# A recurrence with PSUM tiles of its own for even and odd steps, and fewer PSUM banks for the dense products and the preparation

## The chip, the core and the metric

The kernel runs on one NeuronCore of one Trainium2 chip. The metric is device time in microseconds (us) of one execution, inputs and outputs in HBM. The five engines are TensorE (PE, matrix products), VectorE (DVE), ScalarE (ACT), GpSimdE (POOL) and SyncE (SP, which issues DMAs here). Matrix products land in PSUM, which this kernel uses as eight banks of 128 partitions x 512 fp32 values, one tile per bank.

## The reference, cut to what matters

Two requests of 512 tokens and width 1024 go through the same two layers. Layer 0 is dilated window attention beside a Hyena convolution, then a feed-forward layer with a width-3 convolution (`ffn`, 2816 wide). Layer 1 is a bidirectional RWKV-7 recurrence, then another `ffn`. The recurrence is the part that the change is about:

```
def _wkv_scan(r, decay, k, v, kk, a, reverse):
    def step(S, inp):
        r_t, w_t, k_t, v_t, kk_t, a_t = inp
        sa = jnp.einsum('bhvk,bhk->bhv', S, -kk_t)
        S = (S * w_t[:, :, None, :] + sa[..., None] * (kk_t * a_t)[:, :, None, :]
             + v_t[..., None] * k_t[:, :, None, :])
        return S, jnp.einsum('bhvk,bhk->bhv', S, r_t)
...
x = x + g1 * mix
h = _rmsnorm(x, p['norm2']) * (1.0 + sc2) + sh2
x = x + g2 * _conv_ffn(h, p)
```

## The kernel before, in words

The two requests are two Python generators, a (s = 0) and b (s = 1), that are woven by `run` with fixed weights. While a is in its recurrence (`rw_loop`), b supplies dense products, and the other way round. From what the generators issue, a list scheduler makes one fixed order of instructions for each engine; it also decides which bank a tile gets. Instructions of an engine then run in that order, each waiting for what it needs.

**Dense products.** `dense` (L123) loads a block of weights, splits it into a high part (`whi`, an ACT cast, L107) and a low part (`wlo`, a POOL subtraction, L111), and accumulates 9 to 24 matmuls of 128x512 into one PSUM tile `pd`; ACT or DVE then read it. During the loops every three matmuls are followed by a yield, so that the recurrence's matmuls come in between.

**Recurrence.** The 512 tokens of a request are cut into 16 chunks of 32; both directions and up to two pairs of heads advance together. There are 72 steps for each request. A step of `rw_steps` (L1153) is a chain. First the state times the chunk's keys and queries (`X<-S,AR`) and a product of values (`X<-UV,Am`) go to PSUM. ACT takes `xs` from it (L1191), a product with the chunk's inverse (`X<-xs,Am`) follows, ACT takes `UV` (L1201). Then the outputs (`X<-UV,Am`) and the state's update (`X<-UV,TBK`) follow. DVE makes the new `S` from PSUM (L1212), and DVE or ACT copy the step's outputs into `Y` (L1221, L1223). All of this lives in one tile X of two banks: columns 0 to 255 hold the outputs, alternating by halves between even and odd steps, 256 to 383 the inverse's product, 384 to 511 the update. The framework orders two accesses of the same bank by different engines even where the columns differ, so the first product of the next step, `X<-S,AR`, waits for the `Y` copies of this one.

**Preparation.** `rw_front` makes the matrices of the next pair of heads: two PSUM tiles at a time for `Am` (`ps<-AR,BK`, read by DVE, L1075), then two for the transposes `TBK` (`ps<-ident,BK`, read by ACT, L1100). `rw_back` makes the inverse by 31 steps of two DVE instructions (L1125, L1127).

**Projection.** `rw_project` of a request ends in eight rounds (one for each block of 128 channels): a dense product `wv`, then products with low-rank weights, a gate (`ps<-lg1ah`, copied by ACT in L921), a transpose (`ps<-ident,tv`) and small products, each in a PSUM tile of its own. For b the last rounds come when a's loop is over. Its PSUM tiles then come from the same pool as the dense products.

**Banks before.** `psd` has three banks for the dense products, throughout. In mixer 0, `psm` has five. In a loop, `psl` has three and X two.

Of the kernel before, what the change touches and what calls it, by code (L numbers as in the profile page):

```python
# [8 lines left out]
F32 = mybir.dt.float32  # L9
F32R = mybir.dt.float32r  # L10
AF = mybir.ActivationFunctionType
ALU = mybir.AluOpType
AX = mybir.AxisListType
PSUM = bass.MemoryType.PSUM
# [3 lines left out]
L = 512  # L18
# [32 lines left out]
class K:  # L51
    def __init__(self, tc, a, outs):
        self.tc, self.nc, self.a, self.o = tc, tc.nc, a, outs
        self.ctx = ExitStack()
        self.side = ["left", "right"]
        self.grain, self.behind, self.last = KC, False, None

    def pool(self, name, bufs=1, space=None, ctx=None, side=None):
# [5 lines left out]
    def ps(self, name="ps"):  # L64
        pool = self.psm[self.cur] or self.psl or self.psd
        return pool.tile([128, 512], F32, tag="pd" if pool is self.psd else "ps", name=name)

    def v(self, name, i=0, n=1):
# [54 lines left out]
    def dense(self, src, nk, xs, evac, m=128, before=()):  # L123

        wh, wl = self.load_w(src, nk, m)
        ps = self.psd.tile([128, 512], F32, tag="pd", name="pd")
        for k in range(nk):
            self.mm3(ps[:m], (wh[k], wl[k]), xs(k), k == 0, k == nk - 1)
            if (k + 1) % self.grain == 0 and k + 1 < nk:
                yield self.grain * 648  # L130
        yield from before
        evac(ps[:m])
        yield (nk % self.grain or self.grain) * 648
# [13 lines left out]
    def setup(self):  # L147
        nc, a = self.nc, self.a
        self.cp = self.pool("const")
        self.wp = self.pool("w")  # L150
        self.psd = self.pool("psd", bufs=3, space=PSUM)
        self.dp = self.pool("dram", space=DRAM)
# [92 lines left out]
    def stat_end(self, s):  # L245

        nc = self.nc
        yield 3000
        ps = self.psd.tile([128, 512], F32, tag="pd", name="pd")
        for i in range(4):  # L250
            self.mm(ps[:, i:i + 1], self.r[s][:, i * 128:i * 128 + 128], self.ones[:, 0:1], start=True, stop=True)
        m = self.rc[s]
        nc.vector.tensor_scalar(m, ps[:, 0:4], 1.0 / D, 1e-6, ALU.mult, ALU.add)
        nc.gpsimd.tensor_tensor(m, m, self.mhalf[:, 0:4], ALU.pow)
        r3 = self.r[s].rearrange("p (i t) -> p i t", i=4)
        nc.vector.tensor_tensor(r3, self.ident[:, None, :].to_broadcast([128, 4, 128]), m[:, :, None].to_broadcast([128, 4, 128]), ALU.mult)
        yield 3000
        ps = self.psd.tile([128, 512], F32, tag="pd", name="pd")
        self.mm(ps, self.ones, self.r[s], start=True, stop=True)
        nc.scalar.copy(self.r[s], ps)  # L260
        yield 4000
# [177 lines left out]
    def attention(self, s, hs, ap, op, then, early):  # L439

        nc, a = self.nc, self.a
        xs = lambda k: hs[k]
# [8 lines left out]
        def project(g, hp):  # L451
            if hp == 0:
                V[g] = ap.tile([128, 4, 256], F32, tag="V", bufs=2, name="V")
                pv = [self.psd.tile([128, 512], F32, tag="pd", name="pv") for _ in range(2)]
                for i in range(2):
                    wh, wl = self.load_w(a["wva"][g, :, i * 4:i * 4 + 4], 4, 256)
                    for k0 in (0, 2):
                        for b in range(4):
                            o = pv[b // 2][:, b % 2 * 256:b % 2 * 256 + 256]
# [20 lines left out]
        g, hp = parts[-1]  # L480
# [249 lines left out]
    def rw_project(self, s, ctx):  # L730
        nc, a, side = self.nc, self.a, self.side[s]
        sc = lambda key, c: self.rwd[key, s][c]
        mp = self.pool(f"xm{s}", ctx=ctx, side=side)
        hsel = mp.tile([128, 2, 32], F32, name="hsel")
# [4 lines left out]
        o2 = self.pool(f"hid{s}", ctx=ctx, side=side)  # L739
        if s == 0:  # L740
            self.wq[0] = self.pool("wq", ctx=ctx, side=side)
            ctx.callback(lambda: self.wq.pop(0))
        c1 = ctx.enter_context(ExitStack())
        hp = self.pool(f"h1{s}", ctx=c1, side=side)
        o1 = self.pool(f"po{s}", ctx=c1, side=side)
# [14 lines left out]
        xx, xs = [], {}  # L760
# [40 lines left out]
        if s == 0:  # L801
            yield from differences(self.pool(f"xx{s}", ctx=c1, side=side))
        pn = self.psd.tile([128, 512], F32, tag="pd", name="pn")
        yield from mix(2)
# [4 lines left out]
        def k_evac(ps, c):  # L809
            while late:  # L810
                late.pop()()
            t = new("t1")
            nc.scalar.copy(t, ps)
            put("k", c, t)
            sq = new("t1")
            nc.scalar.activation(sq, ps, AF.Square, scale=self.v("kk", c))
            q = slice(c // 2 * 32, c // 2 * 32 + 32)
            late.append(lambda: self.mm(pn[q], hsel[:, c % 2], sq, start=c % 2 == 0, stop=c % 2 == 1))

# [121 lines left out]
    def rw_loop(self, s, ctx):  # L941

        nc, a = self.nc, self.a
        P = lambda n, b=1: self.pool(f"{n}{s}", bufs=b, ctx=ctx, side=self.side[s])
        self.psl = self.psm[s] = self.pool(f"psl{s}", bufs=3, space=PSUM, ctx=ctx, side=self.side[s])
        px = self.pool(f"pxu{s}", bufs=1, space=PSUM, ctx=ctx, side=self.side[s])
# [9 lines left out]
        NW = KC + NCH // WAVE - 1  # L956
        self.X = px.tile([128, 2, 512], F32, name="X")
        nc.vector.memset(self.X, 0.0)
        self.G = rc.tile([128, NW * WAVE, 2, 2], F32, name="G")
# [193 lines left out]
    def rw_steps(self, w, live):  # L1153
        nc, per, X = self.nc, self.per, self.X
        H = [slice(h * 64, h * 64 + 64) for h in range(2)]
# [12 lines left out]
        for i in range(WAVE):  # L1168
# [4 lines left out]
            for st in live:  # L1173
# [3 lines left out]
                us.append((st, m, d, st["c"] % 2, n, n // 2, n % 2))  # L1177
            V0 = tau % 2 * 128
            sv = lambda g: slice(V0 + g * 64, V0 + g * 64 + 64)
            uu = lambda g: slice(256 + g * 64, 320 + g * 64)  # L1180
            ss = lambda g: slice(384 + g * 64, 448 + g * 64)
            for st, m, d, g, n, j, q in us:
# [7 lines left out]
            xs = per.tile([128, 2, 2, 64], F32, tag="xs", bufs=1, name="xs")  # L1190
            nc.scalar.activation(xs, X[:, :, V0:V0 + 128].rearrange("p h (g v) -> p h g v", g=2), AF.Copy, scale=-1.0)  # L1191
            yield PW[6] * (1 if w < KC else PW[8] / 100)
# [18 lines left out]
            S = self.S = per.tile([128, 2, 2, 64], F32, tag="S", bufs=1, name="S")  # L1211
            nc.vector.tensor_tensor(S, X[:, :, 384:512].rearrange("p d (g v) -> p d g v", g=2), self.Sg, ALU.add)  # L1212
            Sg = self.Sg = per.tile([128, 2, 2, 64], F32, tag="Sg", bufs=1, name="Sg")
# [80 lines left out]
    def program(self):  # L1294
        self.setup()
        a, b = ((s, self.thread(s)) for s in range(NS))
        self.filter = self.hyena_filter()
# [11 lines left out]
        self.run((a, "wide", 45), (b, None, PW[0]))  # L1309
        self.run((a, "loop", 66), (b, None, PW[1]))  # L1310
        self.grain, self.behind = GRAIN, BEHIND
        self.run((a, "out1", 480), (b, "loop", PW[14], PW[2]))
        self.run((a, None, PW[3]), (b, "loop", 50))
        self.run((a, None, PW[4]), (b, "out1", 480))
        self.grain, self.behind = KC, False
        self.run((a, "end", PW[5]), (b, "normed", 59))
        self.run((b, "end", 1))
        self.ctx.close()

# [158 lines left out]
```

## Time and profile before

| what | value |
|---|---|
| median of 3 runs (3663.87 to 10453.56) | 3672.75 us |
| the profiled execution | 3673.42 us, span of the profile 3671.6 us |
| PE busy | 3349.3 us, 91% |
| DVE, ACT, POOL busy | 1839.7, 1586.2, 1599.1 us |
| granted TensorE clock, mean | 0.941 |
| recurrence of request a, of request b | about 1640 to 2324 us, 2560 to 3170 us |

Busy times are sums over an engine's instructions; an engine's wait is booked to the instruction that ended last before it. A clock of 1.00 is 2.4 GHz, 0.50 is 1.2 GHz.

### The profile page before, as it was taken

To read this page: it belongs to the slowest core of one execution; us is meant where nothing else is said; L and a number is where in the kernel's file an instruction comes from. 1 tells how busy PE (TensorE), PEld (TensorE's weight loads), DVE (VectorE), ACT (ScalarE), POOL (GpSimd) and SP (SyncE) were. 2 spreads that over 40 slices of the span, in tenths; PEclk is the share of its full clock that TensorE was granted. 3 is DMA by queue.
4 is the path that set the end of the run, shared out by engine and by line. 5 is a ranking of instruction groups with operands and counts; after the bars stand their busy time and mean duration, and the time that the engine had idled before them with its cause. 6 is when DMAs were issued, how large, how long until landed. Compare 5 with 4: busy or idle time off the path is not lost. (4 is left out here: it accounts for less than half of the span.)

```text
span 3671.6 us, 62184 instructions
## 1 busy us (share of the span) xinstructions
PE 3349.3 (91%) x24082; PEld 2390.4 (65%) x24082; DVE 1839.7 (50%) x3373; ACT 1586.2 (43%) x3233; POOL 1599.1 (44%) x1480
## 2 busy tenths in 40 slices
PE   7999999999998989988887888887988889989998
PEld 4555777877876766666665554555656566667776
DVE  5021432122336373577777777567777765442223
ACT  3122344443235445445545557544455454443332
POOL 2111343244446565444444456444444444444443
PEclk9999999999999999899988898798899999999999
DMA  7655231223243326543334331574334432342322
GB/s 247 224 181 198 67 112 64 69 81 122 76 149 115 119 82 207 197 128 95 102 98 134 101 102 48 199 256 129 100 89 106 113 77 83 110 164 89 97 90 88
DMA packets 335519, 450.62 MB, mean 123 GB/s; under 512 B 160023, under 2 KB 177687, under 8 KB 333816
## 3 DMA queue, kind: packets, MB, share of 16 engines
q1 hardware_dynamic: 259664, 235.16, 20.7%
q10 hardware_dynamic: 75560, 211.48, 17.9%
q8 instruction: 190, 3.11, 0.3%
q14 instruction: 105, 0.86, 0.1%
HBM read 373.92 MB, written 72.61 MB: 122 GB/s over the span
## 5 line engine op out<-in xcount | busy, mean ns | idle before, releaser
L111 POOL TENSOR_TENSOR wlo<-wraw,whi 128x512 fp32r<-128x512 f32 (+1 forms) x830 | 1087.5, 1314 | 1424.9 <-ACT whi L107 1218.5
L107 ACT CAST whi<-wraw 128x512 fp32r<-128x512 f32 (+1 forms) x830 | 497.5, 605 | 879.4 <-PE pd L77 648.8
L77 PE MATMUL pd<-midh,whi 128*128 128x512 f32 x704 | 294.7, 420 | 21.0 <-ACT midh L140 20.8
L77 PE MATMUL pd<-midl,whi 128*128 128x512 f32 x704 | 290.3, 413 | 5.3 <-DVE midl L143 4.8
L77 PE MATMUL pd<-midh,wlo 128*128 128x512 f32 x704 | 289.0, 411 | 0.3 <-POOL wlo L111 0.3
L327 DVE SCALAR_TENSOR_TENSOR x<-pd,ada,x 128x512 f32<-128x512 f32 x192 | 143.1, 748 | 209.4 <-PE pd L77 208.6
L77 PE MATMUL pd<-xml,whi 128*128 128x512 f32 (+1 forms) x448 | 194.1, 434 | 22.5 <-DVE xml L143 15.2
L77 PE MATMUL pd<-xmh,whi 128*128 128x512 f32 (+1 forms) x448 | 196.1, 441 | 6.1 <-ACT xmh L140 5.9
L1125 DVE TENSOR_TENSOR sub<-U,W 128x120 f32<-128x120 f32 (+7 forms) x496 | 186.4, 376 | 23.6 <-DMA U<-inv 11.2
L1127 DVE TENSOR_TENSOR W<-W,sub 128x120 f32<-128x120 f32 (+7 forms) x496 | 188.8, 381 | 12.4
L77 PE MATMUL pd<-xmh,wlo 128*128 128x512 f32 (+1 forms) x448 | 190.0, 425 | 1.3 <-POOL wlo L111 1.2
L77 PEld LDWEIGHTS pd<-midh,whi 128*128 128x128 f32 x704 | 136.4, 194 | 56.9 <-ACT midh L140 23.9
L1201 ACT COPY UV<-X 32x128 f32<-32x128 f32 x512 | 131.6, 257 | 85.1 <-PE X L77 54.2
L320 DVE TENSOR_TENSOR fa<-fa,pd 128x512 f32<-128x512 f32 x88 | 60.4, 686 | 214.4 <-PE pd L77 202.8
L290 DVE SCALAR_TENSOR_TENSOR fa<-pd,vecs,fa 128x511 f32<-128x511 f32 x88 | 65.8, 747 | 203.7 <-ACT fa L289 203.0
L1214 POOL TENSOR_TENSOR Sg<-S,G 128x256 f32<-128x256 f32 x144 | 94.7, 658 | 164.2 <-DVE S L1212 153.0
L77 PEld LDWEIGHTS pd<-midl,whi 128*128 128x128 f32 x704 | 137.4, 195 | 40.3 <-DVE midl L143 9.9
L77 PEld LDWEIGHTS pd<-midh,wlo 128*128 128x128 f32 x704 | 137.1, 195 | 32.7 <-POOL wlo L111 1.5
L77 PE MATMUL X<-UV,Am 32*32 32x64 f32 (+1 forms) x4096 | 129.0, 230 | 24.2 <-ACT UV L1201 22.1
L1223 ACT COPY Y<-X 32x128 f32<-32x128 f32 x256 | 65.7, 257 | 180.6 <-DVE Y L1221 98.9
L77 PEld LDWEIGHTS X<-UV,Am 32*32 32x32 f32 (+1 forms) x4096 | 79.9, 110 | 92.5 <-ACT UV L1201 67.1
L77 PE MATMUL X<-S,AR 64*64 64x64 f32 x1920 | 63.4, 241 | 83.9 <-ACT Y L1223 64.0
(474 smaller groups left out, 8066.2 us busy)
## 6 DMA issues: line engine op xcount, KB each, us to landing
wraw<-in_up ACTq DMA_DIRECT2D x176, 512.0 KB, 3.6
adaw<-in_adaw SPq DMA_DIRECT2D x96, 512.0 KB, 5.4
wraw<-in_dn ACTq DMA_DIRECT2D x128, 256.0 KB, 2.7
wraw<-in_win ACTq DMA_DIRECT2D x36, 512.0 KB, 3.7
x<-x SPq DMA_DIRECT2D x48, 256.0 KB, 3.8
wraw<-in_dn ACTq DMA_DIRECT2D x64, 192.0 KB, 2.4
x<-res SPq DMA_DIRECT2D x32, 256.0 KB, 3.0
wraw<-in_wk ACTq DMA_DIRECT2D x16, 512.0 KB, 3.8
```

The source lines that it names most:

```text
L77: return self.nc.tensor.matmul(*a, **k)
L107: nc.scalar.copy(h, raw[:, o:o + w])
L111: nc.gpsimd.tensor_tensor(l, raw[:, o + p:o + p + w2], h[:, p:p + w2].bitcast(F32), ALU.subtract)
L290: nc.vector.scalar_tensor_tensor(t[:, 1:], ps[:, :L - 1], w(0), t[:, 1:], ALU.mult, ALU.add)
L320: nc.vector.tensor_tensor(act, act, ps, ALU.mult)
L327: nc.vector.scalar_tensor_tensor(x[m], ps, self.ada[l][:, 40 + m, s:s + 1], x[m], ALU.mult, ALU.add)
L1125: nc.vector.tensor_tensor(w, U4[:, :, k:, e * K + k:e * K + k + 1].to_broadcast(shape), W4[:, e:e + 1, k:k + 1, 0:k + 1].to_broadcast(shap ...
L1127: nc.vector.tensor_tensor(W4[:, :, k:, 0:k + 1], W4[:, :, k:, 0:k + 1], w, ALU.add)
L1201: nc.scalar.copy(dst, X[ur, :, uu(g)])
L1214: nc.gpsimd.tensor_tensor(Sg, S, self.G[:, tau, :, :, None].to_broadcast([128, 2, 2, 64]), ALU.mult)
L1223: nc.scalar.copy(dst, src)
```

## The change

X becomes two tiles of two banks, used by even and odd steps (`X[tau % 2]`). To pay for these two banks, `psd` goes from three banks to two and `psl` from three to two. A third bank for dense products (`third`, `pd`) exists outside the stretch from the begin of a's loop to the begin of a's last `ffn`; in that stretch there is none. Where that bank is there, the dense products take it in every third turn. `pn`, the sums of squares of eight blocks, no longer keeps a PSUM bank during the `wk` products: it becomes an SBUF tile that is filled from short-lived PSUM tiles, by one ACT copy or one DVE addition of 32x512 for each block. In mixer 0 the two accumulators `pv` come from `psm` instead of `psd`. A pool `psn` of three banks serves request a's projection until its first part ends.

```
     def ps(self, name="ps"):
         pool = self.psm[self.cur] or self.psl or self.psd
...
+    def pd(self):
+        self.turn = (self.turn + 1) % 3
+        if self.psx and self.turn == 0:
+            return self.psx.tile([128, 512], F32, tag="px", name="pd")
+        return self.psd.tile([128, 512], F32, tag="pd", name="pd")
...
-        ps = self.psd.tile([128, 512], F32, tag="pd", name="pd")
+        ps = self.pd()
...
-        self.psd = self.pool("psd", bufs=3, space=PSUM)
+        self.psd = self.pool("psd", bufs=2, space=PSUM)
...
-                pv = [self.psd.tile([128, 512], F32, tag="pd", name="pv") for _ in range(2)]
+                pv = [self.ps("pv") for _ in range(2)]
...
+        self.psm[s] = None if s else self.pool(f"psn{s}", bufs=3, space=PSUM, ctx=c1, side=side)
...
-        pn = self.psd.tile([128, 512], F32, tag="pd", name="pn")
+        pn = o2.tile([128, L], F32, tag="lg1al", bufs=1, name="pn")
...
-            late.append(lambda: self.mm(pn[q], hsel[:, c % 2], sq, start=c % 2 == 0, stop=c % 2 == 1))
+            def norms():
+                p = self.ps()
+                self.mm(p[q], hsel[:, c % 2], sq, start=True, stop=True)
+                if c % 2 == 0:
+                    nc.scalar.copy(pn[q], p[q])
+                else:
+                    nc.vector.tensor_tensor(pn[q], pn[q], p[q], ALU.add)
+            late.append(norms)
...
-        self.psl = self.psm[s] = self.pool(f"psl{s}", bufs=3, space=PSUM, ctx=ctx, side=self.side[s])
+        self.psl = self.psm[s] = self.pool(f"psl{s}", bufs=2, space=PSUM, ctx=ctx, side=self.side[s])
...
-        self.X = px.tile([128, 2, 512], F32, name="X")
-        nc.vector.memset(self.X, 0.0)
+        self.X = [px.tile([128, 2, 512], F32, name=f"X{i}") for i in range(2)]
+        for x in self.X:
+            nc.vector.memset(x, 0.0)
...
-            V0 = tau % 2 * 128
-            sv = lambda g: slice(V0 + g * 64, V0 + g * 64 + 64)
-            uu = lambda g: slice(256 + g * 64, 320 + g * 64)
-            ss = lambda g: slice(384 + g * 64, 448 + g * 64)
+            X = self.X[tau % 2]
+            sv, uu, ss = (lambda g, o=o: slice(o + g * 64, o + g * 64 + 64) for o in (0, 128, 256))
...
         self.run((a, "loop", 66), (b, None, PW[1]))
+        px.close()
         self.grain, self.behind = GRAIN, BEHIND
         self.run((a, "out1", 480), (b, "loop", PW[14], PW[2]))
         self.run((a, None, PW[3]), (b, "loop", 50))
         self.run((a, None, PW[4]), (b, "out1", 480))
         self.grain, self.behind = KC, False
+        px = self.third()
```

The scheduler's order changes with the dependences. On PE, at one step of request b's loop (the 106th of the 142 steps with a previous state), these are the instructions between the state's update `X<-UV,TBK` and the next step's first product `X<-S,AR`; `pd` are dense products, `psq` is a transpose of finished outputs. Before:

```order
L77 MATMUL X<-UV,TBK 64x64 x8
L77 MATMUL pd<-h2h,whi 128x512
L77 MATMUL pd<-h2l,whi 128x512
L77 MATMUL pd<-h2h,wlo 128x512
L80 MATMUL ps<-ident,psq 128x128 x4
L77 MATMUL pd<-h3h,whi 128x512
L77 MATMUL pd<-h3l,whi 128x512
L77 MATMUL X<-S,AR 64x64 x8
```

After, in the same step (X_21431 and X_21432 are the two tiles):

```order
L91 MATMUL X_21431<-UV,TBK 64x64 x8
L91 MATMUL pd<-h0h,whi 128x512
L91 MATMUL pd<-h0l,whi 128x512
L91 MATMUL pd<-h0h,wlo 128x512
L91 MATMUL X_21432<-S,AR 64x64 x8
```

Nine matmuls stood there and three do now. Summed over the 142 places, 1375 matmuls stood between update and next product, and 775 do after the change; the difference stands in front of `X<-xs,Am` and the second `X<-UV,Am` instead.

The second place is on PE in request a's loop, where a new pair of heads is prepared (`ps<-AR,BK` the products for `Am`, `ps<-ident,BK` the transposes for `TBK`). Before, the transposes follow the first half of the products:

```order
L77 MATMUL X<-UV,Am 32x64 x8
L77 MATMUL X<-UV,TBK 64x64 x8
L77 MATMUL pd<-ones,r_103 128x1 x4
L77 MATMUL ps<-AR,BK 64x64 x8
L80 MATMUL ps<-ident,BK 128x128 x4
L77 MATMUL X<-S,AR 64x64 x8
```

After, the first half stands alone there:

```order
L91 MATMUL X_10824<-UV,Am 32x64 x8
L91 MATMUL X_10824<-UV,TBK 64x64 x8
L91 MATMUL pd<-ones,r_103 128x1 x4
L91 MATMUL ps<-AR,BK 64x64 x8
L91 MATMUL X_10823<-S,AR 64x64 x8
```

Its transposes have moved behind the last products of the pair, some 60 rows further on.

## Rows read from the trace of the kernel before

**Rows 1.** Windows of core 0: busy us of each engine (count), clock, DMA share, GB/s

```profile
0.00:1100.00 1100.00, 1062.43 (x4681) 764.85 (x4682) 312.99 (x523) 379.39 (x738) 349.98 (x283) 0.98 0.39 132
...
1640.00:2285.00 645.00, 553.98 (x7029) 369.96 (x7027) 473.64 (x1004) 349.94 (x823) 320.82 (x343) 0.90 0.35 99
...
2324.00:2437.00 113.00, 103.39 (x326) 64.40 (x327) 53.26 (x69) 58.12 (x97) 52.22 (x49) 0.85 0.82 282
...
2560.00:3170.00 610.00, 542.74 (x7186) 373.83 (x7185) 406.25 (x954) 299.32 (x741) 272.54 (x293) 0.95 0.35 94
```

**Rows 2.** Waits of PE over the span: us in total, times, longest us

```profile
PE X L77 <- ACT Y L1223: 64.0, 48, 3.7
PE X L77 <- ACT UV L1201: 22.1, 29, 2.4
...
PE X L77 <- ACT xs L1191: 15.3, 20, 2.9
...
PE ps L77 <- DVE Am L1075: 13.2, 6, 4.5
```

**Rows 3.** Timeline of one step, PE, DVE, ACT: start us, us, instruction, idle before

```profile
2869.66 0.46 PE L77 MATMUL X<-UV,TBK 64*64 64x64 f32 x16
...
2870.39 0.39 PE L77 MATMUL pd<-h2l,whi 128*128 128x512 f32 x1
2870.62 0.39 PE L77 MATMUL pd<-h2h,wlo 128*128 128x512 f32 x1
...
2871.99 0.46 PE L77 MATMUL X<-S,AR 64*64 64x64 f32 x16
...
2870.29 0.42 DVE L1212 TENSOR_TENSOR S<-X,Sg 128x256 f32<-128x256 f32 x1 [1.05 <-PE X L77]
...
2871.41 0.53 ACT L1223 COPY Y<-X 32x128 f32<-32x128 f32 x2 [1.52 <-DVE Y L1221]
```

**Rows 4.** Timeline of the step with one of the longest waits

```profile
2958.19 0.39 PE L77 MATMUL pd<-h2h,whi 128*128 128x512 f32 x1
2962.15 0.46 PE L77 MATMUL X<-S,AR 64*64 64x64 f32 x16 [3.57 <-ACT Y L1223]
...
2960.18 0.28 DVE L1125 TENSOR_TENSOR sub<-U,W 128x120 f32<-128x120 f32 x1
2960.50 0.42 DVE L1212 TENSOR_TENSOR S<-X,Sg 128x256 f32<-128x256 f32 x1
...
2961.58 0.52 ACT L1223 COPY Y<-X 32x128 f32<-32x128 f32 x2 [2.18 <-DVE Y L1221]
```

**Rows 5.** The gate's copies, L921, and the timeline around one (PE, ACT)

```profile
L921 ACT COPY po<-ps x8: 586/587/591, 2342.1 to 2432.1; 128x512 f32<-128x512 f32 x8
...
2404.26 0.51 PE L77 MATMUL pd<-xmh,whi 128*128 128x512 f32 x1
...
2407.01 0.33 ACTq L102 DMA_DIRECT2D wraw<-in_wv  x1
2407.38 0.59 ACT L921 COPY po<-ps 128x512 f32<-128x512 f32 x1 [1.25 <-POOL wlo L111]
```

**Rows 6.** Timeline as request a's loop begins, PE and DVE

```profile
1600.94 0.40 PE L77 MATMUL pd<-h0h,whi 128*128 128x512 f32 x1
...
1614.46 0.39 PE L77 MATMUL pd<-midh,whi 128*128 128x512 f32 x1
...
1604.52 0.74 DVE L291 SCALAR_TENSOR_TENSOR fa<-pd,vecs,fa 128x511 f32<-128x511 f32 x1
...
1619.71 0.74 DVE L291 SCALAR_TENSOR_TENSOR fa<-pd,vecs,fa 128x511 f32<-128x511 f32 x1
```

**Rows 7.** Timeline of a transpose and of the copy that frees its bank

```profile
2007.56 1.11 PE L80 MATMUL ps<-ident,BK 128*128 128x128 f32 x4
...
2027.82 0.37 ACT L1100 COPY TBK<-ps 128x256 f32<-128x256 f32 x1 [0.40 <-PE X L77]
```

**Rows 8.** Window behind a wait of 2.6 us on the Y copies

```profile
2687.00:2690.00 3.00, 3.00 (x19) 2.25 (x12) 0.69 (x1) 1.03 (x4) 1.86 (x2) 0.50 0.96 164
```

More of the change, by code (lines that the diff above doesn't have):

```diff
@@ L56, in __init__ @@
         self.grain, self.behind, self.last = KC, False, None
+        self.turn, self.psx = 0, None
     def pool(self, name, bufs=1, space=None, ctx=None, side=None):
@@ L66, in ps, with third @@
         return pool.tile([128, 512], F32, tag="pd" if pool is self.psd else "ps", name=name)
+    def pd(self):
[3 more added lines that the diff above has]
+        return self.psd.tile([128, 512], F32, tag="pd", name="pd")
+    def third(self):
+        ctx = ExitStack()
+        self.psx = self.pool("psx", space=PSUM, ctx=ctx)
+        ctx.callback(lambda: setattr(self, "psx", None))
+        return ctx
     def v(self, name, i=0, n=1):
@@ L248, in stat_end @@
         yield 3000
-        ps = self.psd.tile([128, 512], F32, tag="pd", name="pd")
+        ps = self.pd()
         for i in range(4):
@@ L257, in stat_end @@
         yield 3000
-        ps = self.psd.tile([128, 512], F32, tag="pd", name="pd")
+        ps = self.pd()
         self.mm(ps, self.ones, self.r[s], start=True, stop=True)
@@ L1153, in rw_steps @@
     def rw_steps(self, w, live):
-        nc, per, X = self.nc, self.per, self.X
+        nc, per = self.nc, self.per
         H = [slice(h * 64, h * 64 + 64) for h in range(2)]
@@ L1190, in rw_steps @@
             xs = per.tile([128, 2, 2, 64], F32, tag="xs", bufs=1, name="xs")
-            nc.scalar.activation(xs, X[:, :, V0:V0 + 128].rearrange("p h (g v) -> p h g v", g=2), AF.Copy, scale=-1.0)
+            nc.scalar.activation(xs, X[:, :, 0:128].rearrange("p h (g v) -> p h g v", g=2), AF.Copy, scale=-1.0)
             yield PW[6] * (1 if w < KC else PW[8] / 100)
@@ L1211, in rw_steps @@
             S = self.S = per.tile([128, 2, 2, 64], F32, tag="S", bufs=1, name="S")
-            nc.vector.tensor_tensor(S, X[:, :, 384:512].rearrange("p d (g v) -> p d g v", g=2), self.Sg, ALU.add)
+            nc.vector.tensor_tensor(S, X[:, :, 256:384].rearrange("p d (g v) -> p d g v", g=2), self.Sg, ALU.add)
             Sg = self.Sg = per.tile([128, 2, 2, 64], F32, tag="Sg", bufs=1, name="Sg")
@@ L1315, in program @@
         self.grain, self.behind = KC, False
+        px = self.third()
         self.run((a, "end", PW[5]), (b, "normed", 59))
         self.run((b, "end", 1))
+        px.close()
         self.ctx.close()
```

## The prediction

> **What bounds the kernel now.** I read the windows by stage first, then PE's waits, then timelines of single places. The windows say that PE is the engine to watch: in the first 1100 us it computes for all but 38 us, in a's loop for 554 of 645 us, in b's for 543 of 610 [rows 1]; DVE and ACT are busy for at most three quarters of either loop. So the change can return only what PE idles, and can take time wherever PE begins to idle. The waits say where it idles inside the loops: 64.0 us in 48 waits for the copies of `Y`, 22.1 us for `UV`, 15.3 us for `xs`, and 13.2 us in 6 waits of the preparation's tiles for DVE's reads of `Am` [rows 2]. These are the only waits that X and `psl` touch directly: 101 us at the chain's three links, less than 3% of the run.
>
> **What a wait for Y is made of.** In a common step the update's products start at 2869.66, DVE has written the new `S` at 2870.29 + 0.42 = 2870.71, and the last copy into `Y` ends at 2871.41 + 0.53 = 2871.94; the next `X<-S,AR` starts 0.05 us later [rows 3]. The change removes the condition on `Y`, since the next step writes another tile. The condition on `S` stays. In such a step that is 2871.94 − 2870.71 = 1.23 us of freedom. In a long wait it looks otherwise: PE idles 3.57 us before 2962.15, but `S` itself is ready only at 2960.50 + 0.42 = 2960.92, since DVE was in an instruction of the inverse (`sub`, until 2960.46) [rows 4]. Only 2962.10 − 2960.92 = 1.18 of the 3.57 us is the fault of `Y`. A third of the wait leaves, and two thirds get another name.
>
> The Trainium skill ("PSUM — Partial Sum Buffer", section "Summary: rules for kernel authors") says that a matmul should go to a different bank than the one being read. By that rule alone the 64.0 us would go whole. The sum below with 64 in place of 20 would be 3655 us; rows 4 speak against it, because `S` is late there as well.
>
> **What the scheduler does with the freedom.** The order lists show that it spends most of it. The matmuls between update and next product fall from 1375 to 775. One more matmul of 128x512 in a row takes 2870.62 − 2870.39 = 0.23 us [rows 3]. So 600 × 0.23 = 138 us of cover leave this place, 0.97 us for each of the 142 links, and the wait shrinks against 1.23 us by only 0.26. That alone would leave a gain of 64 × 0.26/1.23 = 13 us; the single long wait gives 64 × 1.18/3.57 = 21. **I take −20**, nearer to the long waits because they hold most of the 64 us; bounds −12 and −64.
>
> The 138 us of cover go in front of the products that wait for `xs` and `UV`: 0.49 us for each of 284 links. Those links wait 37.4 us in 49 waits, 0.76 us each [rows 2]. If the new cover stood at these very places, two thirds would go, but most links don't wait at all and need no cover. **I take −12**, a third; bounds 0 and −37.
>
> **What the banks cost.** (1) b's eight rounds of `wv`, 2324 to 2437 us, run when a's loop is over. All their PSUM tiles come from `psd`, which has two banks now; the two of `psl` and the four of X lie unused. PE is busy for 103 of these 113 us [rows 1]. Each round has one tile of the gate, read by an ACT copy (L921, 8 of them) that comes late: ACT waits 1.25 us for POOL's `wlo` ahead of it and has a DMA issue and casts in front. With three banks the next dense product starts at 2404.26, while that copy still is to come and ends at 2407.38 + 0.59 = 2407.97 [rows 5]. With two banks this product needs the very bank that the copy reads: 3.71 us for PE. Seven of the eight copies have a dense product behind them: 7 × 3.71 = **+26 us**. The lower end is 0, if the scheduler's order brings the copies forward.
>
> (2) Such waits also bring the clock down. After a wait of 2.6 us on `Y` the next 3 us run at 0.50, 1.2 GHz, instead of 2.4 [rows 8], which loses 1.5 us. Seven times that is 10; the stretch is at 0.85 on average already [rows 1], so some of the loss is there anyway: **+5**, from 0 to 10.
>
> The Trainium skill ("TensorE: Matmul & The Clock Gate", section "A second HAM failure mode: psum-queue depth-cycling") describes a kernel whose pauses between groups, as it cycles through PSUM banks, lost clock. By it every one of the seven waits would cost the whole, 10 instead of 5, and the sum would be 3704; rows 8 show the same behind one wait.
>
> (3) As a's loop begins, the `ffn`'s dense products of b run beside it. Two of them start at 1600.94 and 1614.46 while DVE's read of an earlier tile (L291) ends at 1604.52 + 0.74 and 1619.71 + 0.74 [rows 6]. If each had to wait for that read, it would be 4.32 + 5.99 = 10.3 us, and the beginning of b's loop could cost as much again, 21 in all. The recurrence's own matmuls can fill part of these waits only where they stand ahead in PE's fixed order. **I take +14**, two thirds.
>
> (4) `psl` has two banks instead of three. The pair of `Am` tiles fills both, and the next pair, the transposes and `psq` wait for DVE's read. This wait exists already with three banks, 13.2 us [rows 2]. **I take +13**, as much again; from 0 to 26 (twice as much).
>
> (5) The rest counts as nothing. The eight copies and eight additions of `pn` (32x512) lie on ACT and DVE, which idle for a third or more of the time; if the cover were gone, with the 0.5 to 0.6 us of a copy [rows 3, 5] they would cost 16 × 0.6 = 10 us. The second X is one more memset before each loop, off PE. `pv` in `psm` leaves mixer 0, where PE hardly idles, with five banks for two long-lived tiles and the rest; dense products get a third bank there. For these I allow 10 us either way.
>
> **The sum.** −20 − 12 + 26 + 5 + 14 + 13 = +26 us. The profiled execution took 3673.4 us (its span 3671.6), 0.7 above the median of the three runs. So 3673.4 + 26 = **3699 us**.
>
> **The rivals.**
>
> *The chain is what counted, and it gets free (faster).* `S` is on time in most of the 48 waits, the long one shown is an exception, and the cover moved to `xs` and `UV` fills these links too. Then −64 − 37, and seven of the longest waits no longer pull the clock down, −10; the dense products of the loops find their banks free, and only the `wv` rounds cost, +31. 3673 − 111 + 31 = 3593 us. It decides if DVE stands idle ahead of `S` in most of the waits. For it speaks the common step [rows 3], where DVE had waited for PE; against it the long step [rows 4] and the order, which takes 0.97 of the 1.23 us back.
>
> *The preparation starves (slower).* The transposes for `TBK` are done on PE at 2007.56 + 1.11, and the copy that frees the bank ends only at 2027.82 + 0.37 [rows 7]: the bank is held for 20 us, because ACT may not write `TBK` before the old pair's last step has read it. With three banks two are left during such a hold; with two, only one, for pairs that want two, and for `psq`. If PE reaches such a tile in the middle of a hold, it waits for 10 us, with the recurrence queued behind it. Eight such places in both loops make 80 us: 3699 + 80 = 3779. It decides where products or transposes of the preparation stand on PE between the transposes and that copy. The scheduler knows of the hold and has moved the transposes behind the pair's last products in the place shown, which speaks against it.
>
> *The banks cost little (no change).* The gate's copies come earlier in the new order, so that the `wv` rounds are as before, and all else is as in the sum: 3673 − 32 + 27 = 3668. For it: ACT is busy for only 53 of those 113 us [rows 1]. Against it: the copy waits for POOL, which has not become faster.
>
> **How the numbers follow.** The forecast has 50%, with a range of its own from 3675 to 3735: the `wv` rounds between 10 and 36 us, (3) and (4) between 10 and 47, the gains between 12 and 45. The faster rival has 15%, the slower one 17%, no change 18%. A change of 2%, 73 us, is about what a measurement of this kernel can tell from none. Below 3599 us lies about half of the faster rival: 0.08. Above 3746 lies the slower rival but a little: 0.16, with 0.01 for the forecast's tail: 0.17. Within 2% stays 0.75. The range leaves out most of the faster rival (some 13%) and the upper third of the slower one (some 6%): 3630 to 3770.
>
> **What would show it right or wrong.** In the profile of the changed kernel PE's wait for `Y` at L1223's successor is gone, and `X<-S,AR` waits instead for DVE's `S`, with 35 to 50 us in all; below 20 the first rival is right. The waits for `xs` and `UV` together should be near 25 us, the wait for `Am` near 26. Between the end of a's loop and the beginning of b's, PE waits for the gate's copy on ACT, seven times by 2 to 6 us, and the `wv` rounds take some 30 us longer at a clock below 0.85; if they take 113 us as before, the third rival is right. Waits of 5 us and more for ACT's `TBK` copy within the loops would show the second one. If the first 1100 us differ by more than 10 us, the mixer's banks were misjudged.

## The result, and the profile after

The changed kernel takes 3699.48 us (median of 4 runs, 3698.92 to 3701.76), the kernel before 3668.31 us (median of 4, one of which took 10453.56 us and is left out of the ratio): a ratio of 1.0093, with a 95% interval from 1.0071 to 1.0114. Forecast were 3699 us. The sum is right to the microsecond, but several of its terms are not: no gain came where 32 us were expected, and the losses were less than half of what was written down. That these errors balance so closely is luck.

The profiled execution has a span of 3697.1 us, 25.5 more than before. The windows by stage say where they lie. The stages end at the first and last product of X in each loop (a's loop begins at 1606 us by this, not at about 1640); columns as in [rows 1]. Before:

```profile
1606.30:2315.60 709.30, 600.52 (x7396) 399.65 (x7395) 520.01 (x1089) 381.75 (x883) 354.45 (x374) 0.89 0.35 96
...
2315.60:2528.20 212.60, 181.58 (x767) 120.62 (x764) 120.98 (x178) 98.05 (x167) 102.25 (x99) 0.85 0.68 228
...
2528.20:3169.40 641.20, 566.50 (x7363) 391.63 (x7362) 435.68 (x1018) 312.23 (x762) 287.26 (x307) 0.95 0.35 94
3169.40:3671.60 502.20, 469.74 (x1985) 370.31 (x1979) 176.59 (x231) 176.14 (x292) 223.16 (x178) 0.97 0.34 108
```

After:

```profile
1614.70:2327.80 713.10, 598.88 (x7388) 398.62 (x7389) 503.95 (x1078) 379.10 (x878) 345.68 (x369) 0.89 0.34 95
...
2327.80:2555.00 227.20, 187.77 (x766) 122.43 (x761) 120.02 (x185) 99.52 (x170) 103.75 (x101) 0.85 0.64 213
...
2555.00:3183.90 628.90, 556.70 (x7343) 382.74 (x7344) 431.11 (x1013) 311.06 (x762) 283.57 (x305) 0.95 0.35 96
3183.90:3697.10 513.20, 477.45 (x2009) 375.31 (x2004) 179.09 (x233) 178.35 (x296) 224.83 (x180) 0.97 0.33 107
```

Request a's loop begins 8.4 us later. The two loops together are 8.5 us shorter (1350.5 to 1342.0), but PE also did 11.4 us less work in them (1167.0 to 1155.6); 7.7 us of that work turn up behind the second loop, which is 11.0 us longer. Between the loops, where the rounds of `wv` stand, 14.6 us were added. 8.4 − 8.5 + 14.6 + 11.0 = 25.5 us.

The waits of PE, over the span, after the change:

```profile
PE X L91 <- DVE S L1234: 65.8, 47, 3.7
PE X L91 <- ACT xs L1213: 20.8, 35, 2.7
...
PE ps L91 <- DVE Am L1099: 19.6, 11, 6.0
PE X L91 <- ACT UV L1223: 17.3, 21, 2.4
...
PE pd L91 <- DVE fa L305: 9.9, 6, 4.3
...
PE pd L91 <- ACT midh L154: 9.1, 5, 4.4
...
PE pd L91 <- ACT po L944: 6.2, 7, 1.1
...
PE pd L91 <- DVE fa L334: 2.8, 1, 2.8
...
PE ps L94 <- DVE Am L1099: 1.1, 1, 1.1
```

Beside [rows 2] the reader sees the main finding. The wait for `Y`, 64.0 us, is gone, and 65.8 us for `S` stand in its place. `xs` and `UV` together had 37.4 us and have 38.1. The wait for `Am` grew from 13.2 to 20.7 (19.6 ahead of products, 1.1 ahead of transposes), and the gate's copy (`po`) is waited for seven times, as forecast, but for 6.2 us in all. Two rows of before, not shown so far, belong to the lines `fa` and `midh`:

```profile
PE pd L77 <- ACT midh L140: 20.8, 8, 9.5
...
PE pd L77 <- DVE fa L291: 2.2, 1, 2.2
```

One of the long waits for `S`, in the timeline after the change:

```profile
2830.32 0.46 PE L91 MATMUL X<-UV,TBK 64*64 64x64 f32 x16
...
2830.72 2.28 DVE L1055 TENSOR_TENSOR_SCAN ld_sg<-smask,ld_sg 128x512 f32<-128x512 bf16 x1 [1.38 <-DMA ld_sg<-sg]
...
2832.92 1.68 DVE L157 TENSOR_TENSOR midl<-fa,midh 128x512 fp32r<-128x512 f32 x1
...
2834.53 0.28 DVE L1149 TENSOR_TENSOR sub<-U,W 128x132 f32<-128x132 f32 x1
...
2835.40 0.42 DVE L1234 TENSOR_TENSOR S<-X,Sg 128x256 f32<-128x256 f32 x1
...
2835.87 0.70 PE L91 MATMUL X<-S,AR 64*64 64x64 f32 x16 [3.73 <-DVE S L1234]
```

The update ends at 2830.78, and `S` could be made at once. But five other instructions stand ahead of it in DVE's fixed order: a scan that had itself waited 1.38 us for a DMA, a `midl` of a dense product, and three of the inverse, one of them shown here. `S` begins 4.6 us late. This is the rule and not the exception: of the 43 places after the change where PE stands for more than 0.3 us ahead of `X<-S,AR`, DVE had something else still to finish at 38 when the update ended; at 24 of them `sub` or `W` of the inverse stands directly ahead of `S`. `S` begins a median of 2.47 us after the update's end at the 43 places, and 0.17 us at the other 99.

### The profile page after: what moved, and what is told of

It is laid out like the page before. It is cut to its first block, busy times and chain, and to the rows that moved or that the text cites. A ratio compares the mean times of both kernels' runs of the same rounds, so it can differ in the third digit from the quotient of the medians.

```text
span 3697.1 us, 62085 instructions
## 1 busy us (share of the span) xinstructions
PE 3350.9 (91%) x24082; PEld 2390.7 (65%) x24082; DVE 1828.5 (49%) x3383; ACT 1590.9 (43%) x3243; POOL 1585.6 (43%) x1480
## 5 line engine op out<-in xcount | busy, mean ns | idle before, releaser
L1151 DVE TENSOR_TENSOR W<-W,sub 128x120 f32<-128x120 f32 (+7 forms) x496 | 175.3, 354 | 11.7
L304 DVE SCALAR_TENSOR_TENSOR fa<-pd,vecs,fa 128x511 f32<-128x511 f32 x88 | 65.8, 748 | 198.7 <-ACT fa L303 198.3
L91 PEld LDWEIGHTS pd<-midh,wlo 128*128 128x128 f32 x704 | 135.8, 193 | 31.4 <-issue 0.4
L1245 ACT COPY Y<-X 32x128 f32<-32x128 f32 x256 | 65.8, 257 | 189.5 <-DVE Y L1243 113.0
L91 PEld LDWEIGHTS pd<-xmh,whi 128*128 128x128 f32 (+1 forms) x448 | 91.5, 204 | 66.4 <-ACT xmh L154 26.2
```

What stands on the lines that cost most here:

```text
L91: return self.nc.tensor.matmul(*a, **k)
L304: nc.vector.scalar_tensor_tensor(t[:, 1:], ps[:, :L - 1], w(0), t[:, 1:], ALU.mult, ALU.add)
L1151: nc.vector.tensor_tensor(W4[:, :, k:, 0:k + 1], W4[:, :, k:, 0:k + 1], w, ALU.add)
L1245: nc.scalar.copy(dst, src)
```

## The experiments

**One X again, with the banks of the change.** This separates the banks from the split.

```
-        self.X = [px.tile([128, 2, 512], F32, name=f"X{i}") for i in range(2)]
+        self.X = [px.tile([128, 2, 512], F32, name="X")]
...
-            X = self.X[tau % 2]
-            sv, uu, ss = (lambda g, o=o: slice(o + g * 64, o + g * 64 + 64) for o in (0, 128, 256))
+            X, V0 = self.X[0], tau % 2 * 128
+            sv, uu, ss = (lambda g, o=o: slice(o + g * 64, o + g * 64 + 64) for o in (V0, 256, 384))
```

> The change with a single X tile of two banks for all steps (outputs alternate by columns as before the change); the other two banks of X lie unused, everything else, the two banks of psd and psl too, is as after the change. It tells the price of the banks from the gain of the split. By the prediction's sum (gain 32 us, price 58 us) it takes 3699 + 32 = 3731 us. By the rival that the profile of the changed kernel suggests (PE waits 65.8 us for DVE's S where it waited 64.0 us for the copies of Y, so the split gained next to nothing) it takes 3700 us, within 8 us.

Measured: 3680.0 us, ratio 1.0021 (1.0004 to 1.0038). Neither theory had it. The banks, with all else of the change but the split, cost some 8 us, not 58, and the split on top of them doesn't gain 32 but costs: 1.0093 − 1.0021 is 0.7%, 26 us (24 by the second measurement of the change, below). PE waits 62.8 us for `Y` here, where it waits 65.8 for `S` with two tiles:

```profile
PE X L91 <- ACT Y L1245: 62.8, 55, 3.8
```

**The unused banks given to the `wv` rounds.**

```
         for c in range(KC):
+            if s and not self.psl and not self.psm[s]:
+                self.psm[s] = self.pool("psg", bufs=5, space=PSUM, ctx=ctx, side=side)
+                ctx.enter_context(self.third())
             t = new("tv")
```

> The change, but b's rounds of wv between the two loops get the six banks that lie unused there: five for the small products and a third one for the dense products. It tells whether the banks are what makes the stretch between the loops longer. In the changed kernel that stretch (end of a's loop to the first product of b's) takes 227 us, before 213. If the banks are the cause, it takes about 213 again and the kernel about 3685 us, and the waits for the gate's copy (seven, 6.2 us) are gone. If the cause is the order of the filling work (less of it left over for the stretch), the kernel stays at 3700 us, within 5 us.

Measured: 3665.18 us, ratio 0.9986 (0.9967 to 1.0005), 37 to 39 us below the change by the ratios. The stretch between the loops is 206 us long (before 213, the change 227), and no wait for the gate's copy is left. So the banks there are a cause, as the first theory said. In the profiles, which are 37.8 us apart, 21 us are all that this stretch gives; a's loop begins 6.7 us sooner, the loops are 8.1 us shorter; more on the rest below. The eight copies of the gate mark the rounds. After the change, from the first to the last:

```profile
L944 ACT COPY po<-ps x8: 580/586/586, 2356.1 to 2460.5; 128x512 f32<-128x512 f32 x8
```

and with the added banks:

```profile
L947 ACT COPY po<-ps x8: 578/584/592, 2343.0 to 2432.3; 128x512 f32<-128x512 f32 x8
```

104.4 us against 89.3; before they took 90.0 [rows 5].

**DVE's order: S ahead of the inverse**, in the change and in the kernel before.

```
-            nc.vector.tensor_tensor(S, X[:, :, 256:384].rearrange("p d (g v) -> p d g v", g=2), self.Sg, ALU.add)
+            self.newS = nc.vector.tensor_tensor(S, X[:, :, 256:384].rearrange("p d (g v) -> p d g v", g=2), self.Sg, ALU.add)
...
-            nc.vector.tensor_tensor(w, U4[:, :, k:, e * K + k:e * K + k + 1].to_broadcast(shape),
+            i = nc.vector.tensor_tensor(w, U4[:, :, k:, e * K + k:e * K + k + 1].to_broadcast(shape),
                                     W4[:, e:e + 1, k:k + 1, 0:k + 1].to_broadcast(shape), ALU.mult)
+            if self.newS:
+                self.after(i, self.newS)
```

> The change, with one more condition on the order of instructions: on DVE an instruction of the inverse (sub) that comes later in the program may not be put ahead of the state S. No work is added. It tells why S is late. If S is late because DVE sits in the inverse (24 of the 43 longer waits of the changed kernel have sub or W ahead of S), the waits for S fall from 66 us to below 45 and the kernel to about 3680 us. If the wait is there because PE has too little work between the update and the next product, whenever DVE begins, they stay at 66 us and the time at 3700 us.

> The kernel before with the same condition on DVE's order. If DVE's lateness is what both kernels wait for, the waits for Y fall here as well, from 64 us to about 45, and the kernel takes about 3653 us; if the copies of Y were a limit of their own, they stay above 55 us and the time within 8 us of 3671.

Measured: 3715.16 us, ratio 1.0122 (1.0092 to 1.0153), and for the kernel before 3770.92 us, ratio 1.0277 (1.0246 to 1.0308). The waits of PE with the split X:

```profile
PE X L91 <- DVE S L1236: 36.4, 36, 2.5
PE ps L91 <- DVE BK L1082: 31.6, 8, 6.2
PE X L91 <- ACT UV L1225: 29.0, 32, 5.9
```

The first half of the theory holds: `S` comes sooner and its waits fall from 65.8 to 36.4 us. The second doesn't: the time rose. `BK` of the preparation, which had no such row after the change, is waited for 31.6 us now, and the two loops take 1392.6 us instead of 1342.0; that the preparation is late because it gives way to `S` is the likely reason, though not shown. In the kernel before, the waits for ACT's copies of `Y` fell only from 64.0 to 53.9 us, and those for DVE's additions to `Y` rose from 2.4 to 14.1, so that `Y` is waited for as long as before; the waits for `psq` rose from 7.8 to 31.4 us. This order, at least, doesn't put DVE's lateness away.

**The change once more, and one bank more in the `wv` rounds.** The third bank of `third` is opened for b's rounds alone, and `ps` takes its turns in it too.

```
         pool = self.psm[self.cur] or self.psl or self.psd
+        if pool is self.psd and self.cur == 1 and self.psx and self.behind:
+            return self.pd()
...
         for c in range(KC):
+            if s and not self.psl and not self.psx:
+                ctx.enter_context(self.third())
```

> The changed kernel itself once more, on the same chip as the three that follow, so that they can be set against it. Every theory expects a ratio to the kernel before near 1.009.

> The change with one more bank only in b's wv rounds, taken in turns by dense and small products: three in all, as many as before the change had there. It tells whether the loss against before is the step from three to two in that stretch. If so, it comes back to about 3675 us; if the split's order is at fault and the six banks of gap_banks only covered it, it stays near 3690 us.

Measured: 3698.72 us, ratio 1.0086 (1.0054 to 1.0118), for the change, and 3678.7 us, ratio 1.0028 (1.0010 to 1.0046), with three banks in the rounds. The row of the gate's copies with three:

```profile
L948 ACT COPY po<-pd x8: 585/586/589, 2343.4 to 2437.7; 128x512 f32<-128x512 f32 x8
```

94.3 us, against 104.4 and 107.2 in the two profiles of the change. So 10 to 13 us of the 20 are the third bank in these rounds. The other part isn't there. The two loops are 6 and 12 us longer in this profile (1348.0 against 1342.0 and 1335.6), and a's loop begins sooner: at 1614.7 and 1617.3 us in the two profiles of the change, at 1608.0 with six added banks and 1604.6 with one. Ahead of the loops the order of the instructions on all engines is the same in these kernels, up to 1590 us. The rows of one stretch before that, of the change (first two), of the kernels with six and one more banks, and of two other kernels with this order: the one with two tiles in "DVE relieved" below, which has the six banks too, and the change with `S` ahead of the inverse:

```profile
1390.00:1540.00 150.00, 149.67 (x491) 104.93 (x490) 54.29 (x73) 72.03 (x114) 64.98 (x60) 0.83 0.58 197
...
1390.00:1540.00 150.00, 147.70 (x482) 103.03 (x483) 51.74 (x70) 73.65 (x116) 64.53 (x60) 0.83 0.58 196
...
1390.00:1540.00 150.00, 145.57 (x521) 99.08 (x521) 59.04 (x80) 77.29 (x122) 70.13 (x65) 0.93 0.63 211
...
1390.00:1540.00 150.00, 145.63 (x531) 100.69 (x529) 60.11 (x84) 77.11 (x123) 70.18 (x65) 0.94 0.63 214
...
1390.00:1540.00 150.00, 149.68 (x493) 104.45 (x492) 53.77 (x71) 70.82 (x113) 64.79 (x60) 0.84 0.58 194
...
1390.00:1540.00 150.00, 145.95 (x538) 100.22 (x537) 61.98 (x85) 79.78 (x126) 73.19 (x67) 0.95 0.65 218
```

PE is busy for 97% or more in all six, but the granted clock is 0.83 or 0.84 in three and 0.93 to 0.95 in the others, which get through 521 to 538 instructions instead of 482 to 493. The low clock isn't the mark of the change: a kernel with the added banks has it, and others of the same order don't. The four profiles of the kernel before and its variants, which share an order of their own here, lie between 0.90 and 0.97. So the later begin of a's loop differs between executions of one order, and no run shows that the banks or the split bring it. What makes the clock differ stays open.

**One X with the added banks, and the kernel before with added banks.** The first is one_x with the edit of gap_banks, the second has the pool `psg` of five banks but no `third`, since `psd` has three anyway.

> One X tile for all steps, as in one_x, and the six unused banks given to b's rounds of wv, as in gap_banks. If the price of the banks in that stretch is its own thing, it takes one_x less the 15 us that the stretch is longer there, about 3665 us, and the split of X gains nothing beside it (gap_banks took 3665 us). If the split gains in the loops what the prediction gave it (32 us) and gap_banks shows it, this kernel takes 3697 us.

> The kernel before, with the five banks that lie unused between the loops given to the small products of b's wv rounds; three stay for the dense products. It tells whether the kernel before already lost time to its three banks there. PE idles for about 14 of 121 us in that stretch before. If banks are part of it, some 5 to 10 us leave (3665 us); if it is the chain of the small products and the casts alone, nothing does (3672 us).

Measured: 3657.54 us, ratio 0.9971 (0.9955 to 0.9987), and 3662.94 us, ratio 0.9985 (0.9968 to 1.0002). The first is faster than the kernel before and than the change. Against gap_banks, which differs by the split alone, it is 0.9971 to 0.9986: with the banks paid for, the split of X changes nothing that can be measured, or costs 5 us. The two loops together take 1336.9 us with one tile and 1333.9 with two, and what is behind them 502.6 (3649.0 − 3146.4) and 511.3 (3659.3 − 3148.0). The 3 us in the loops are less than the 6.4 us by which two profiles of the change differ there; the 9 us behind them are filling work that was left for later. PE is busy for 1160.9 us in the loops with one tile and for 1148.3 with two, so that it idles there for 176.0 us with one and for 185.6 with two. The waits of PE with two tiles, and with one, say where:

```profile
PE X L91 <- DVE S L1237: 63.4, 50, 3.1
PE X L91 <- ACT xs L1216: 25.1, 36, 5.2
...
PE ps L91 <- DVE Am L1102: 20.2, 10, 5.9
...
PE X L91 <- DMA Am<-inv: 11.3, 5, 3.1
```

```profile
PE X L91 <- ACT Y L1248: 63.4, 54, 4.2
...
PE X L91 <- ACT xs L1216: 14.4, 19, 2.9
...
PE ps L91 <- DVE Am L1102: 12.2, 5, 6.5
...
PE X L91 <- DVE Y L1246: 8.0, 5, 3.2
...
PE X L91 <- DMA Am<-inv: 3.2, 3, 1.6
```

`S` is waited for as long as ACT's copies were. The split saves the waits for DVE's additions to `Y`, 8.0 us, but `xs`, `Am` and the DMA that brings the inverse into `Am` are waited for 26.8 us more; other rows give part of that back. Of the 24 to 26 us that the split seems to cost on top of one_x, the work left for later (11 us in the profiles) and the later begin of a's loop, 1604.3 to 1614.7, are most; the second goes with the clock of that stretch and may be no cost of the split. The rounds of `wv` with one tile and the added banks, and those of one_x:

```profile
L947 ACT COPY po<-ps x8: 577/584/587, 2335.5 to 2423.7; 128x512 f32<-128x512 f32 x8
```

```profile
L944 ACT COPY po<-ps x8: 579/579/587, 2331.3 to 2440.5; 128x512 f32<-128x512 f32 x8
```

88.2 us against 109.2: 21 us, as much as the 18 us (by the ratios) between the two kernels. The kernel before gained about 6 us from its own five idle banks, not clear of none by its interval; its rounds take 82.5 us instead of 90.0.

**DVE relieved.** Only 7 of the 31 steps of the inverse, with two X tiles and with one, both with the added banks; the other 24 steps are left out.

```
-        for j in range(C - 1):
+        for j in range(7):
```

> The change with the six banks of gap_banks, and only 7 of the 31 steps of the inverse: the other 24 (48 instructions of DVE for each pair of heads) are left out. To be set against one_cut alone. It tells what the split is worth where DVE has time. If S was late because DVE was busy, the waits for S fall from 63 us to below 30, and the kernel is at least 15 us faster than one_cut. If the scheduler's order eats the gain whatever DVE does, the two stay within 8 us of one another.

> One X for all steps with the banks of one_x_gap, and only 7 of the 31 steps of the inverse; the other 24 are left out. Here the copies of Y remain a condition of the next step. If DVE was what both waited for, PE's waits for Y fall less than those for S in split_cut, to 35 to 50 us; if the order of the filling work decides, they are as long as those of split_cut.

Measured: 3535.08 us, ratio 0.9621 (0.9573 to 0.9669), with two tiles, 3551.99 us, ratio 0.9683 (0.9648 to 0.9717), with one. The wait at the link, with two tiles and with one:

```profile
PE X L91 <- DVE S L1237: 39.2, 26, 3.0
```

```profile
PE X L91 <- ACT Y L1248: 50.3, 44, 4.1
```

Now the split is worth 17 us, though the two intervals overlap by a little. In the profiles the loops are 40.8 us shorter with two tiles (1208.8 against 1249.6), and about half of that comes back outside them. The waits for `S` fell from 63.4 us in gap_banks to 39.2, less than to the 30 that were expected: at 16 of its 25 longer waits DVE is in something other than what is left of the inverse. At these 25 places `S` is as late as before, by a median of 2.51 us; but there are fewer of them than the 44 of gap_banks. With one tile `Y` still costs 50.3. So the split gains something once `S` is late less often, which speaks for DVE as what keeps the gain away in the whole kernel. That DVE's time alone does it isn't shown, since the order on all engines changes with the instructions left out.

**Two banks in `psl`, alone.**

```
-        self.psl = self.psm[s] = self.pool(f"psl{s}", bufs=3, space=PSUM, ctx=ctx, side=self.side[s])
+        self.psl = self.psm[s] = self.pool(f"psl{s}", bufs=2, space=PSUM, ctx=ctx, side=self.side[s])
```

> The kernel before with two banks in psl instead of three, nothing else. The prediction gave this edit +13 us (3682 us in all), with the waits for DVE's Am near 26 us. In one_x, which has two banks in psl and two in psd, b's loop took 629 us where it took 641 before. If psl is what made that loop shorter, the time is about 3660 us and b's loop below 635; if the dense products' banks did it, the time is 3668 to 3685 and b's loop 641 or longer.

Measured: 3680.0 us, ratio 1.0024 (1.0002 to 1.0046): 9 us more, where the prediction had 13. Only a little of it is the wait that it named: `Am` is waited for 10.9 us ahead of products and 4.6 ahead of transposes here, 15.5 in all, and 13.2 before.

```profile
PE ps L77 <- DVE Am L1075: 10.9, 5, 4.5
...
PE ps L80 <- DVE Am L1075: 4.6, 3, 1.9
```

The loss is in a's loop, 724.7 us (before 709.3), while b's is shorter, 635.6 (before 641.2). What else makes it isn't shown.

**A third bank for the dense products within the loops**, with one X. The `px.close()` ahead of the loops and the `third()` behind them are taken out of one_x_gap.

> One X for all steps as in one_x_gap, with the third bank for dense products kept through both loops, since a single X leaves it free, and five banks for the small products between the loops. One_x_gap took 3657.5 us. If dense products wait for their banks inside the loops as the prediction said (10 us at each begin of a loop), it takes about 3645 us; if two banks are enough there, it stays within 6 us of one_x_gap.

Measured: 3675.94 us, ratio 1.0019 (1.0003 to 1.0036). A bank more makes the kernel 18 us slower; neither theory had that. Both loops are longer, 717.5 and 642.8 us against 706.3 and 630.6. One place shows a part of it, the waits of PE from 1590 to 1700 us, as a's loop begins. With the third bank:

```profile
PE pd L91 <- ACT midh L154: 9.5, 1, 9.5
```

and with two:

```profile
PE pd L91 <- DVE fa L305: 4.6, 1, 4.6
PE pd L91 <- ACT midh L154: 3.3, 1, 3.3
```

The wait for the bank (`fa`, 4.6 us) is the one that the prediction took from [rows 6] at 4.32 us, and it came. But a wait of 9.5 us for the operand of a later product stood there with three banks, in the kernel before too, and it shrank to 3.3. The bank's wait is for the most part time that PE would have stood before that product anyway. That is 1.6 us in favour of two banks. The rest isn't mainly waiting: in the profiles the two loops are 23.4 us longer with the third bank, and of these PE idles for only 6.2 us more (182.2 against 176.0). It is busy for 17.2 us more, for 26 more records of 14744, at a clock of 0.87 and 0.94 in the two loops instead of 0.88 and 0.95. The cause isn't settled.

## Why the sum was right and its terms were not

- **The wait for Y (−20): wrong, by its size.** It went, as forecast, and `S` took its place, as forecast, with 65.8 us instead of 35 to 50. The long step [rows 4] had been read rightly: `S` late behind the inverse. So had the order: the time from the update's end to the next product shrank by a mean of 1.00 us (2.83 to 1.83), about the 0.97 us that the prediction worked out for each link, though only some 450 of the 600 moved matmuls are of 128x512, for which its price of 0.23 us holds. What failed was the step from there to the gain. The 13 us came from the freedom of a common step, 1.23 us [rows 3], but common steps don't wait. The 21 us, to which the term was set nearer, took the 1.18 us of the long step whole and didn't subtract the moved cover from it. With it 1.18 − 0.97 = 0.21 us of 3.57 is left, which is 4 us of the 64 and near the nothing that came. In the steps that wait after the change, DVE is late by a median of 2.5 us, and less cover stands in front of it: what `Y` gave back the scheduler had already spent. The Trainium skill's rule ("PSUM — Partial Sum Buffer", section "Summary: rules for kernel authors") would have brought 64 us: of the wait for the bank it is right, which went whole, and of the time the measurement decides.
- **xs and UV (−12): wrong.** 37.4 to 38.1 us. The 0.49 us of cover per link didn't shorten these waits; with the same banks the split even raises those for `xs`, 14.4 to 25.1 us. The faster rival fell with these two; its condition, DVE idle ahead of `S`, held at 5 of the 43 places after the change.
- **The `wv` rounds (+26, and +5 for the clock): right in place and kind, wrong in size.** Seven waits for the gate's copy came, of 0.9 us on the average instead of 3.71 [rows 5]. The step that failed was to take the copy's lateness from the old order. The copies in the view by lines (busy us, mean ns, then the idle time of ACT just before them), before and after:

```profile
L921 ACT COPY po<-ps 128x512 f32<-128x512 f32 x8 | 4.7, 587 | 9.2 <-POOL wlo L111 5.9 <-DMA sg<-po 2.0 <-POOL whi L918 1.4
...
L944 ACT COPY po<-ps 128x512 f32<-128x512 f32 x8 | 4.7, 584 | 0.0
```

  ACT stood 9.2 us ahead of them and stands 0.0 now, as the new order puts the copy where nothing holds ACT up. This is the third rival's mechanism. The rounds still grew from 90.0 to 104.4 us: PE waits 6.2 us for the gate's copy in them and 4.6 for `tv` and `kl` ahead of small products, where no such row stood before. With six more banks they take 88 to 89. The clock's term didn't come: 0.85 between the loops before and after; from the first gate's copy to the last 0.92 before, 0.93 and 0.88 in the two profiles of the change. What the Trainium skill tells of a kernel that cycles through PSUM banks ("TensorE: Matmul & The Clock Gate", section "A second HAM failure mode: psum-queue depth-cycling") isn't seen at these seven waits of a microsecond.
- **The loops' beginnings (+14): wrong, nothing came.** Waits for `fa` grew from 2.2 to 12.7 us (9.9 and 2.8 for two lines), about as priced, and those for `midh` shrank from 20.8 to 9.1: −1 us together. The sum looked only at the wait that would come and not at the one behind it.
- **Am (+13): right in kind, half the size.** 13.2 to 20.7 us after the change. With `psl` alone 9 us were lost, only 2 of them in this wait. The slower rival, a starving preparation, didn't come.
- **The rest (0): within its 10 us** where the mixers are concerned: the last dense product of the first mixers begins at 1075.6 before, and at 1072.9 and 1075.3 in the two profiles of the change. That a's loop begins 8.4 us later goes with the clock behind them, 0.83 where the kernel before had 0.90. No term held it, and it differs as much between executions of one order.

So of +26 us, −32 became +2.5 (`S` for `Y` 1.8, `xs` and `UV` 0.7) and +58 became about 21 (the `wv` rounds 14, `Am` 7, `fa` and `midh` together −1), and the clock ahead of the loops added some 8 in this profile. These are sums of waits and stretches that overlap, so they don't add up to the 25.5 us exactly. The losses written too high hid the two gains that failed. The path was right, that `S` follows `Y` and that the banks cost time in the `wv` rounds; the agreement of the sum is luck.

## What to carry to other kernels

When a change takes one condition of a wait away, look at the next one at the places that do wait, not in a common step; its lateness, set against the cover that the scheduler moves away, decides what is gained. A bank's price has to be read in the stretch where banks are fewest and not where the change is meant to help: here six idle banks, given to a stretch between the loops, were worth 18 us to the kernel with one X, while the split itself was worth nothing until DVE had less to do. And a wait that a smaller pool brings may be only the beginning of one that is there already.

## What the runs showed of the hardware

A stretch of 150 us with PE busy for 97% or more ran at a granted clock of 0.83 or 0.84 in three profiles and at 0.93 to 0.95 in three others, with the same order of instructions up to there. Among the kernels with the whole inverse the start of a's loop moves by up to 13 us with it (1604.6 to 1617.3), as much as most of the terms of this prediction. More PSUM banks for the same work made the kernel slower by 18 us in one place and faster by 18 in another.
